# Keys of U between the steps of the expert choice, the second gathered block's stages first, and a third row buffer: one decoder layer on one core

## The chip, the core and the metric

The kernel runs on one core of one Trainium2 chip. Its time is that of one execution on the device, in microseconds (us); lower is better. The times come from repeated runs, and one further execution was recorded by the hardware profiler. The engines are named as in the profile: PE (TensorE, matmul), PEld (its weight loads), DVE (VectorE), ACT (ScalarE), POOL (GpSimd) and SP (SyncE, which here only issues transfers).

## The reference

The layer takes 512 tokens of width 2048 through three sublayers, each with a residual and a layer norm. The first mixes two sequence models (a gated linear recurrence and a forgetting attention), the second attends to a memory of 256 rows, and the third, which matters here, picks 16 of 16384 experts for each token in each of 8 heads:

```python
q = (x @ w_pq).reshape(B, S, PEER_HEADS, 2, PEER_DK // 2)
sc = jnp.einsum('bshpd,hpnd->bshpn', q, sub_keys)
top_s, top_i = lax.top_k(sc, PEER_TOPK)
...
best_s, best_pos = lax.top_k(cand_s, PEER_TOPK)
idx = jnp.take_along_axis(cand_i, best_pos, -1)
g = jax.nn.softmax(best_s, -1)
...
u = expert_u[it]
a = jnp.einsum('tkd,td->tk', u, xt)
hact = jax.nn.gelu(a, approximate=False) * gt
return jnp.einsum('tk,tkd->td', hact, expert_v[it])
```

An expert's number is made of two indices of 0 to 127: an expert is a pair of sub-keys. Each token has 128 expert rows of U and 128 of V. All data are float32.

## The kernel before, in words

**Blocks.** The 512 tokens are four blocks of 128. Block 0 goes through the whole layer's first two sublayers alone and ahead of the others; blocks 1 to 3 go through the first sublayer together. After that block 1 is taken by the object `e1` and blocks 2 and 3 by `e2` (class `Ends`: `residual`, `norm`, `attend`).

**Matrix products.** All weights come from HBM in pieces of 128 x 2048 float32, 1 MiB, loaded by `load_raw` (L150) on SP's queue into tiles named `raw`. `split_w` (L157) cuts such a piece in two halves. For each, ACT copies the half to a rounded `whi` (L147) and DVE takes the rest, `wlo` (L148); PE multiplies by both. So each half costs one copy on ACT, one split on DVE, and PE cannot start it before both.

**Two ways through the experts.** Blocks 0 and 1 are *gathered*: for each of the 128 experts of each token, POOL issues an indirect transfer of one row per token (`gather`, L981, its instruction at L983) into a `rows` tile of 128 x 2048, 1 MiB. DVE multiplies a row of U with the token and sums (L1006), or adds a row of V times its gate to the accumulator `gacc` (L1020). That makes 256 gathers per block. Tiles `rows` come from `rows_tile`, two buffers in turn. Blocks 2 and 3 are *dense*: PE multiplies all of U with the 256 tokens, one of 128 keys at a time (`stage_a`, L1249: a key is the 128 experts that share one sub-key; its result after the gelu is a tile `ga`), ACT and DVE multiply with a table of gates (`stage_h`), and PE multiplies with all of V (`stage_o`, two halves of 1024 columns for every 8 keys).

**How gathers are put in.** `add_jobs` lists the 256 jobs of a block, and `tick`, called at each split of a weight half, gives credit for a number of PE units, `set_rate` having set the jobs per unit. A job issues its gather; the gather waits for the split at which it was released (`pace`), and its use by DVE is placed `lag` splits later (`after`). Only splits release gathers: where no weights come, no gather starts.

**The stages at the end of the program**, in the order of the code: `e1.residual`, `e1.norm`, `e2.residual`, `e1.attend`, `e2.norm`, `e1.residual`, `e2.attend`, `e1.norm`, `e2.residual`; the choice of experts for block 1 (`pick1`); block 1's jobs are added with a rate of 256 in 1070 units; `e2.norm`; the choice for blocks 2 and 3 (`Choice` with `topk`, 16 pieces of weights, then sorting steps on DVE: L876 to L918); the gate table (`gbuild`, L1208 to L1240: from the chosen indices `i0T`, `i1T` DVE makes 0/1 tiles `o1` and `o0` at L1226 and L1229, ACT scales `o0` by the gate at L1232, PE multiplies them at L1233, ACT copies the product to `stage` at L1236 and stores it to HBM as `gd`); then the dense stage. In it `LOOK` = 32 keys of U run ahead of the first piece of V; after that keys and pieces of V take turns (`ahead`). Of the `ga` tiles 26 are kept; a key that runs further ahead is spilled to HBM (`gad`, 35 keys) and read back (`gb`).

**What sets the order.** The program is built with a scheduler that simulates the engines and orders each engine's instructions by it; the order of the code is only its starting point. On the chip every engine then follows its own list.

Of the kernel before, what the change touches and what calls it, by code (L numbers as in the profile page):

```python
# [21 lines left out]
P = 128  # L22
# [20 lines left out]
J = 8  # L43
GB = 8
LOOK = 32
# [4 lines left out]
def build(tc, I, out):  # L50
    nc = tc.nc
    NC_ = PKEYS
    with ExitStack() as ctx:
# [90 lines left out]
        raws = {"n": 0, "pools": [wp]}  # L144
# [5 lines left out]
        def load_raw(src, n=2048):  # L150
            raws["n"] += 1
            p = raws["pools"][raws["n"] % len(raws["pools"])]
            raw = p.tile([P, 2048], F32, tag="raw", bufs=2, name=nm("raw"))
            nc.sync.dma_start(raw[:, :n], src)
            return raw
# [709 lines left out]
        class Choice:  # L865
# [65 lines left out]
            def run(self, X2, ld):  # L931
                tp, nb = self.tp, self.nb
                for g in range(4):
# [17 lines left out]
                    for t in range(nb):  # L951
# [9 lines left out]
                        nc.scalar.copy(sc, bank)  # L961
                        self.select(t, 2 * g, sc)
# [15 lines left out]
        def rows_tile(n):  # L978
            return gat["pool"].tile([P, D], F32, tag="rows", bufs=2, name=nm(n))
# [185 lines left out]
        X1b, X1c, X2b, X2, PTb, PTc = [], [], [], [], [], []  # L1165
        drain(e1.residual(Gb, I["w_out"], True))
        e1.norm(0, X1b, pr1, False)
        drain(e2.residual(Gc, I["w_out"], True))
# [9 lines left out]
        e1.norm(1, X2b, pr1, True)  # L1178
        drain(e2.residual(PTc, Bv, False))
        with pool("pick1", side="right") as pp:  # L1180
            c = Choice(pp, pp, 1)
            drain(c.run(X2b, nc.sync))
            c.indices(1)
# [3 lines left out]
        set_rate(1070.0)  # L1187
# [4 lines left out]
        gap = ctx.enter_context(pool("gap"))  # L1192
        pre = ExitStack()
# [7 lines left out]
        def a_bank():  # L1201
            return ps.tile([P, 512], F32, tag="s2", bufs=2, name=nm("pa"))
# [8 lines left out]
        for t in range(HB):  # L1211
# [6 lines left out]
            for half in range(2):  # L1218
                stage = [gp.tile([P, 64, 64], F32, tag="stage", bufs=2, name=nm("stage")) for _ in range(2)]
                for q in range(16):  # L1220
# [10 lines left out]
                    for u in range(4):  # L1231
                        nc.scalar.activation(o0[:, u], o0[:, u], AF.Copy, scale=selT["g"][:, ta + u:ta + u + 1])  # L1232
                        nc.tensor.matmul(bank[:, u * P:(u + 1) * P], o1[:, u], o0[:, u], start=True, stop=True)  # L1233
                    bv = bank.rearrange("p (t c) -> p c t", t=4)
# [10 lines left out]
        raws["pools"].append(mn)  # L1245
        acc = [mn.tile([P, D], F32, tag=f"acc{t}", name=f"acc{t}") for t in range(HB)]
        gas, hs, gates = {}, {}, [None]

        def stage_a(c):  # L1249

            bank = a_bank()
            raw = load_raw(I["uT"][c])
            for kt in range(2):
                uh, ul = split_w(raw, kt, 2.1)
                for kk in range(8):
                    k = kt * 8 + kk
                    sl = slice(kk * P, (kk + 1) * P)
                    xh, xl = X2[k]
                    nc.tensor.matmul(bank[:, :H], uh[:, sl], xh, start=k == 0, stop=False)  # L1259
                    nc.tensor.matmul(bank[:, :H], uh[:, sl], xl, start=False, stop=False)  # L1260
                for kk in range(8):
                    k = kt * 8 + kk
                    sl = slice(kk * P, (kk + 1) * P)
                    nc.tensor.matmul(bank[:, :H], ul[:, sl], X2[k][0], start=False, stop=k == 15)  # L1264
            ga = gap.tile([P, H], F32, tag="ga", bufs=GA, name=nm("ga"))
            nc.scalar.activation(ga, bank[:, :H], AF.Gelu)
            if c in spilled:
                nc.scalar.dma_start(gad[c], ga)
            else:
                gas[c] = ga  # L1270
# [79 lines left out]
        ahead = [min(NC_, LOOK + -(-c * (NC_ - LOOK) // (NC_ - J))) for c in range(NC_)]  # L1350
        spilled = {a for c in range(NC_) for a in range(ahead[c - 1] if c else 0, ahead[c]) if a - c >= GA - 1}
# [90 lines left out]
```

## Time and profile before

| what | value |
|---|---|
| median of 3 runs | 5246.53 us (5245.74 to 5247.54) |
| the profiled execution's time | 5243.36 us |
| its span, first to last instruction | 5241.7 us |
| PE busy, share of the span | 4565.4 us, 87% |
| DVE busy | 3915.7 us, 75% |
| ACT busy | 2272.1 us, 43% |
| POOL busy | 811.7 us, 15% |
| moved by DMA | 1479.10 MB, 282 GB/s in the mean |

A busy time is read together with its place: the page's slices cut the span in 40 parts of 131 us and give the busy share in tenths. Stretches can be cut as one likes, and the waits say for whom an engine stood still. Idle time counts only on the engine that the others wait for.

### The profile page before, as it was taken

What the parts mean: (1) busy time and instruction counts of PE and PEld (TensorE: products, weight loads), DVE (VectorE), ACT (ScalarE), POOL (GpSimd) and SP (SyncE); (2) the same over time, 40 slices, a digit from 0 to 9 for tenths busy, and PEclk for the clock granted to TensorE, in tenths of its full rate; (3) what the DMA queues carried; (4) which work ended last, traced back from release to release, by engine and by line L of the source; (5) the groups of instructions that cost most, each with busy time, mean ns of one, the idle gap of its engine ahead of it and who ended that gap; (6) DMA issues with size and microseconds to landing.
All of it is one profiled execution on the core that took longest, in us unless ns stands there. A gap on an engine that the chain in (4) does not pass through costs nothing. (4 is left out here: it accounts for less than half of the span.)

```text
span 5241.7 us, 66469 instructions
## 1 busy us (share of the span) xinstructions
PE 4565.4 (87%) x25662; PEld 4021.7 (77%) x25662; DVE 3915.7 (75%) x5122; ACT 2272.1 (43%) x3129; POOL 811.7 (15%) x631
## 2 busy tenths in 40 slices
PE   7999999789999999999978887369999999999700
PEld 5888888567888998888956667359999999999600
DVE  6877777687776667776778789847787888888755
ACT  5766666543333223333334653364444444444200
POOL 0000000002222222122221001002111121212221
PEclk9999999899999999999989999689999999999955
DMA  7888888557777887776878657159998888888767
GB/s 251 307 316 316 312 314 313 207 201 267 276 272 260 309 306 283 270 276 242 312 273 338 224 209 277 49 167 341 337 337 337 338 333 336 338 332 342 272 243 253
DMA packets 265792, 1479.10 MB, mean 282 GB/s; under 512 B 26845, under 2 KB 73757, under 8 KB 97921
## 3 DMA queue, kind: packets, MB, share of 16 engines
q1 hardware_dynamic: 141696, 884.67, 45.5%
q0 software_dynamic: 81664, 561.95, 28.8%
q10 hardware_dynamic: 42112, 28.22, 1.8%
q8 instruction: 201, 3.29, 0.2%
q14 instruction: 119, 0.97, 0.0%
HBM read 1421.35 MB, written 53.39 MB: 281 GB/s over the span
## 5 line engine op out<-in xcount | busy, mean ns | idle before, releaser
L147 ACT CAST whi<-raw 128x1024 fp32r<-128x1024 f32 x1312 | 1369.4, 1051 | 1785.2 <-PE mm L179 578.4
L148 DVE TENSOR_TENSOR wlo<-raw,whi 128x1024 fp32r<-128x1024 f32 x1312 | 1590.5, 1221 | 552.4 <-ACT whi L147 423.1
L1020 DVE SCALAR_TENSOR_TENSOR gacc<-rows,dots,gacc 128x2048 f32<-128x2048 f32 x256 | 600.8, 2347 | 239.4 <-DMA rows<-in_peer_v,ei 239.0
L1006 DVE SCALAR_TENSOR_TENSOR rows<-rows,x2l 128x2048 f32<-128x2048 f32 x256 | 585.2, 2286 | 171.0 <-DMA rows<-in_peer_u,ei 170.8
L983 POOL DMA_INDIRECT rows<-in_peer_u,ei x256 | 355.3, 1388 | 1943.2 <-DVE rows L1006 755.0
L983 POOL DMA_INDIRECT rows<-in_peer_v,ei x256 | 389.8, 1523 | 1406.4 <-DVE gacc L1020 891.2
L1259 PE MATMUL pa<-Xh,whi 128*128 128x256 f32 x2048 | 503.9, 283 | 32.0 <-ACT whi L147 21.1
L1260 PE MATMUL pa<-Xl,whi 128*128 128x256 f32 x2048 | 503.2, 283 | 0.0
L179 PE MATMUL mm<-Ah,whi 128*128 128x384 f32 x1280 | 439.6, 344 | 8.2 <-DVE qk L612 3.0
L179 PE MATMUL mm<-Al,whi 128*128 128x384 f32 x1280 | 435.6, 341 | 0.0
L147 ACT CAST vh<-raw 128x1024 fp32r<-128x1024 f32 x256 | 268.1, 1052 | 353.1 <-PE mm L1311 331.0
L1259 PEld LDWEIGHTS pa<-Xh,whi 128*128 128x128 f32 x2048 | 389.9, 190 | 39.4 <-ACT whi L147 21.5
L1310 PE MATMUL mm<-vh,hph 128*128 128x512 f32 x1024 | 400.6, 392 | 0.4 <-DVE acc L1332 0.3
L1311 PE MATMUL mm<-vh,hpl 128*128 128x512 f32 x1024 | 400.6, 391 | 0.0
L1260 PEld LDWEIGHTS pa<-Xl,whi 128*128 128x128 f32 x2048 | 388.8, 190 | 6.5
L148 DVE TENSOR_TENSOR vl<-raw,vh 128x1024 fp32r<-128x1024 f32 x256 | 310.6, 1221 | 102.0 <-ACT vh L147 81.8
L223 PE MATMUL mm<-whi,Zh 128*128 128x512 f32 x832 | 333.9, 401 | 48.1 <-ACT whi L147 45.9
L224 PE MATMUL mm<-whi,Zl 128*128 128x512 f32 x832 | 331.2, 398 | 1.1 <-DVE Zl L148 1.1
L223 PE MATMUL mm<-whi,Ah 128*128 128x512 f32 x768 | 314.2, 410 | 7.5 <-ACT whi L147 7.5
L224 PE MATMUL mm<-whi,Al 128*128 128x512 f32 x768 | 311.8, 406 | 0.0
L1316 PE MATMUL mm<-vl,hph 128*128 128x512 f32 x1024 | 281.3, 392 | 9.1 <-DVE vl L148 9.1
L1264 PE MATMUL pa<-Xh,wlo 128*128 128x256 f32 x2048 | 288.7, 282 | 0.0
(399 smaller groups left out, 8360.1 us busy)
## 6 DMA issues: line engine op xcount, KB each, us to landing
raw<-in_w_in SPq DMA_DIRECT2D x256, 1024.0 KB, 5.4
raw<-in_uT SPq DMA_DIRECT2D x128, 1024.0 KB, 6.9
raw<-in_vD SPq DMA_DIRECT2D x128, 1024.0 KB, 6.7
raw<-in_w_out SPq DMA_DIRECT2D x48, 1024.0 KB, 6.2
raw<-in_peer_wq SPq DMA_DIRECT2D x48, 1024.0 KB, 4.8
raw<-in_w_xkv SPq DMA_DIRECT2D x32, 1024.0 KB, 5.6
raw<-in_w_br_ml SPq DMA_DIRECT2D x32, 1024.0 KB, 5.0
raw<-in_w_br_fx SPq DMA_DIRECT2D x32, 1024.0 KB, 4.9
```

The costliest lines, as they stand in the source:

```text
L147: nc.scalar.copy(hi, src)
L148: return nc.vector.tensor_sub(lo, src, hi.bitcast(F32))
L179: i = nc.tensor.matmul(o, w, x, start=start and s % per == 0, stop=stop and s % per == per - 1)
L223: nc.tensor.matmul(banks[t], xh[:, tt], wh[:, c], start=k == 0, stop=False)
L224: nc.tensor.matmul(banks[t], xl[:, tt], wh[:, c], start=False, stop=False)
L983: i = nc.gpsimd.indirect_dma_start(out=rows, out_offset=None, in_=I[table], in_offset=bass.IndirectOffsetOnAxis(ap=ei[t][:, k:k + 1], axis=0))
L1006: i = nc.vector.scalar_tensor_tensor(rows, rows, 1.0, tok[t]["x2l"], op0=ALU.mult, op1=ALU.mult, accum_out=d[:, k % GB:k % GB + 1])
L1020: i = nc.vector.scalar_tensor_tensor(acc, rows, d[:, GB + k % GB:GB + k % GB + 1], acc, op0=ALU.mult, op1=ALU.add)
L1259: nc.tensor.matmul(bank[:, :H], uh[:, sl], xh, start=k == 0, stop=False)
L1260: nc.tensor.matmul(bank[:, :H], uh[:, sl], xl, start=False, stop=False)
L1310: nc.tensor.matmul(banks[t][g], a[:, tt], vh[:, gs_], start=c == c0, stop=False)
L1311: nc.tensor.matmul(banks[t][g], b[:, tt], vh[:, gs_], start=False, stop=False)
```

## The change

The change has five parts.

1. The stages of block 1 come first: `e1.attend` is mixed with `e2.residual`, and `pick1` with `e2.attend`. Block 1's jobs are added ahead of the last `e2.residual`, with 1095 units in place of 1070.
2. The choice for blocks 2 and 3 stops after each of its 8 score tiles (`yield "s"`), and three keys of U (`next_a`) are put in there: 24 keys.
3. In the gate table one key is put in after every fourth of the 64 steps: 16 keys.
4. `LOOK` is 44 in place of 32, so four keys are left to run ahead after the table; 64 keys are spilled in place of 35.
5. In the dense stage every third `rows` tile comes from a third buffer in the pool `main`; in return that pool has one `raw` buffer in place of two, three in all in place of four.

```diff
-LOOK = 32
+LOOK = 44
...
-            raw = p.tile([P, 2048], F32, tag="raw", bufs=2, name=nm("raw"))
+            raw = p.tile([P, 2048], F32, tag="raw", bufs=raws["bufs"][p is not wp], name=nm("raw"))
...
                         nc.scalar.copy(sc, bank)
+                        yield "s"
                         self.select(t, 2 * g, sc)
...
         def rows_tile(n):
+            gat["n"] = gat.get("n", 0) + 1
+            if "more" in gat and gat["n"] % 3 == 0:
+                return gat["more"].tile([P, D], F32, tag="rows", bufs=1, name=nm(n))
             return gat["pool"].tile([P, D], F32, tag="rows", bufs=2, name=nm(n))
...
+        def take(g, n):
+            for _ in range(n):
+                next(g, 0)
+
         drain(e1.residual(Gb, I["w_out"], True))
         e1.norm(0, X1b, pr1, False)
-        drain(e2.residual(Gc, I["w_out"], True))
+        res = e2.residual(Gc, I["w_out"], True)
+        take(res, 4)
+        mix(e1.attend(X1b, pr1, PTb), res, 1)
+        take(res, 2)
+        drain(e1.residual(PTb, Bv, False))
+        e1.norm(1, X2b, pr1, True)
+        drain(res)
         big.close()
...
-        drain(e1.attend(X1b, pr1, PTb))
         e2.norm(0, X1c, lambda: pair(cpl, "X", 16), False)
-        drain(e1.residual(PTb, Bv, False))
-        drain(e2.attend(X1c, pr1, PTc))
+        att = e2.attend(X1c, pr1, PTc)
+        take(att, 2)
+        with pool("pick1", side="right") as pp:
+            c = Choice(pp, pp, 1)
+            mix(c.run(X2b, nc.sync), att, 4)
+            c.indices(1)
+        drain(att)
         cs.close()
...
         add_jobs(1)
-        set_rate(1070.0)
+        set_rate(1095.0)
+        drain(e2.residual(PTc, Bv, False))
         e2.norm(1, X2, lambda: pair(fpl, "X", 16), True)
...
+        def next_a():
+            stage_a(at[0])
+            at[0] += 1
...
-            drain(c.run(X2, nc.sync))
+            for w in c.run(X2, nc.sync):
+                if w == "s":
+                    for _ in range(3):
+                        next_a()
...
+                    if q % 4 == 3:
+                        next_a()
...
-        raws["pools"].append(mn)
+        gat["more"] = mn
+        raws["bufs"] = (2, 1)
+        raws["pools"] = [wp, wp, mn]
...
-        for a in range(ahead[0]):
-            stage_a(a)
+        while at[0] < ahead[0]:
+            next_a()
```

`stage_a` itself is only moved up in the code, with the tables `ahead` and `spilled`. Lines from 960 on have new numbers: L1006 and L1020 are L1010 and L1024, L1332 is L1362.

The three places below show DVE's list of instructions, before and after. DVE in the choice for blocks 2 and 3 before: only sorting steps stand there (`v`, `ix`, `rep` are the best values, their places and a copy without them; `eq` picks indices).

```order
L881 MAX_INDEX ix_25786<-v_25785,rep_25795 128x8
L879 MATCH_REPLACE rep_25801<-v_25785,sc_25783 128x128
L914 TENSOR_TENSOR eq_25769<-eq_25769,ixf_25746 128x512
L879 MATCH_REPLACE rep_25807<-v_25785,sc_25783 128x128
L880 MAX v_25785<-rep_25801 128x8
L915 TENSOR_REDUCE sel_i_4571_25073<-eq_25769 128x32
```

The same place on DVE after the change:

```order
L1010 SCALAR_TENSOR_TENSOR rows_29136,dots_29302<-rows_29136,x2l_24638 128x2048
L914 TENSOR_TENSOR eq_27911<-eq_27911,ixf_27884 128x512
L894 CAST ixf_28141<-ix_28116 128x64
L876 MAX b_28145<-cand_28143 128x8 x2
L148 TENSOR_TENSOR wlo_29395<-raw_29392,whi_29394 128x1024
L148 TENSOR_TENSOR wlo_29425<-raw_29392,whi_29424 128x1024
L915 TENSOR_REDUCE sel_i_4583_25100<-eq_27911 128x32
L1024 SCALAR_TENSOR_TENSOR gacc_24683<-rows_29272,dots_26201,gacc_24683 128x2048
```

Splits of U's keys (`wlo`) and uses of gathered rows have come between the sorting steps: from block 1's indices to the table's start DVE has 118 splits and 59 uses of rows, where it had 21 and 15.

DVE at the end of the gate table before: behind the last 0/1 tiles come the splits of U's keys, which run ahead of V.

```order
L1229 TENSOR_TENSOR o_5038_27583<-i0T,iota 128x512
L1226 TENSOR_TENSOR o_5040_27596<-i1T,iota 128x512
L1229 TENSOR_TENSOR o_5041_27598<-i0T,iota 128x512
L148 TENSOR_TENSOR wlo_27687<-raw_27684,whi_27686 128x1024
L148 TENSOR_TENSOR wlo_27715<-raw_27684,whi_27714 128x1024
L1283 TENSOR_TENSOR ga_27681<-ga_27681,G_29690 128x256
```

The same place on DVE after the change:

```order
L1278 TENSOR_TENSOR o_5359_30120<-i0T,iota 128x512
L1275 TENSOR_TENSOR o_5361_30133<-i1T,iota 128x512
L1278 TENSOR_TENSOR o_5362_30135<-i0T,iota 128x512
L1313 TENSOR_TENSOR ga_25427<-ga_25427,G_30493 128x256
L1313 TENSOR_TENSOR ga_25491<-ga_25491,G_30493 128x256
L148 TENSOR_TENSOR wlo_30290<-raw_30287,whi_30289 128x1024
```

The keys that ran ahead here are gone from this place: 77 more splits of keys stand ahead of the table's first rows and three within its first part; between the last of these and its end there is neither a split nor a gathered row, as before.

DVE around the last pieces of V before (`vl` is the split of V; `acc` the dense blocks' sum):

```order
L1006 SCALAR_TENSOR_TENSOR rows_37753,dots_37192<-rows_37753,x2l_25146 128x2048
L148 TENSOR_TENSOR vl_41672<-raw_41669,vh_41671 128x1024
L148 TENSOR_TENSOR vl_41688<-raw_41669,vh_41687 128x1024
L1020 SCALAR_TENSOR_TENSOR gacc_25209<-rows_37808,dots_36312,gacc_25209 128x2048
L1332 TENSOR_TENSOR acc_27617<-acc_27617,mm_41563 128x512
L1006 SCALAR_TENSOR_TENSOR rows_37866,dots_37192<-rows_37866,x2l_25146 128x2048
```

The same place on DVE after the change:

```order
L148 TENSOR_TENSOR vl_41759<-raw_41756,vh_41758 128x1024
L148 TENSOR_TENSOR vl_41775<-raw_41756,vh_41774 128x1024
L1362 TENSOR_TENSOR acc_30219<-acc_30219,mm_41650 128x512
L1362 TENSOR_TENSOR acc_30219<-acc_30219,mm_41651 128x512
L1362 TENSOR_TENSOR acc_30220<-acc_30220,mm_41652 128x512
L1362 TENSOR_TENSOR acc_30220<-acc_30220,mm_41653 128x512
```

Before, 63 uses of gathered rows stood behind the last split of V. Now none does: all 512 stand ahead of it, 195 of them behind the gate table (241 before).

More of the change, by code (lines that the diff above doesn't have):

```diff
@@ L143, in build @@
         ticks = []
-        raws = {"n": 0, "pools": [wp]}
+        raws = {"n": 0, "pools": [wp], "bufs": (2, 2)}
         def split(hi, lo, src):
@@ L1171, in build @@
         cpl = cs.enter_context(pool("x1c", side="right"))
-        drain(e1.attend(X1b, pr1, PTb))
         e2.norm(0, X1c, lambda: pair(cpl, "X", 16), False)
-        drain(e1.residual(PTb, Bv, False))
-        drain(e2.attend(X1c, pr1, PTc))
+        att = e2.attend(X1c, pr1, PTc)
[5 more added lines that the diff above has]
+        drain(att)
         cs.close()
         fpl = ctx.enter_context(pool("x2c", side="right"))
[L1178 to L1183, printed above, removed]
         while state["done"] < len(jobs):
@@ L1192, in build, with a_bank, stage_a @@
         gap = ctx.enter_context(pool("gap"))
+        gas, at = {}, [0]
+        def a_bank():
+            return ps.tile([P, 512], F32, tag="s2", bufs=2, name=nm("pa"))
+        ahead = [min(NC_, LOOK + -(-c * (NC_ - LOOK) // (NC_ - J))) for c in range(NC_)]
+        spilled = {a for c in range(NC_) for a in range(ahead[c - 1] if c else 0, ahead[c]) if a - c >= GA - 1}
+        def stage_a(c):
+            bank = a_bank()
+            raw = load_raw(I["uT"][c])
+            for kt in range(2):
+                uh, ul = split_w(raw, kt, 2.1)
+                for kk in range(8):
+                    k = kt * 8 + kk
+                    sl = slice(kk * P, (kk + 1) * P)
+                    xh, xl = X2[k]
+                    nc.tensor.matmul(bank[:, :H], uh[:, sl], xh, start=k == 0, stop=False)
+                    nc.tensor.matmul(bank[:, :H], uh[:, sl], xl, start=False, stop=False)
+                for kk in range(8):
+                    k = kt * 8 + kk
+                    sl = slice(kk * P, (kk + 1) * P)
+                    nc.tensor.matmul(bank[:, :H], ul[:, sl], X2[k][0], start=False, stop=k == 15)
+            ga = gap.tile([P, H], F32, tag="ga", bufs=GA, name=nm("ga"))
+            nc.scalar.activation(ga, bank[:, :H], AF.Gelu)
+            if c in spilled:
+                nc.scalar.dma_start(gad[c], ga)
+            else:
+                gas[c] = ga
+        def next_a():
+            stage_a(at[0])
+            at[0] += 1
         pre = ExitStack()
@@ L1196, in build @@
             c = Choice(pp, tp, 2)
-            drain(c.run(X2, nc.sync))
+            for w in c.run(X2, nc.sync):
+                if w == "s":
+                    for _ in range(3):
+                        next_a()
         sel = c.sel
         state["lag"] = 3
-        def a_bank():
-            return ps.tile([P, 512], F32, tag="s2", bufs=2, name=nm("pa"))
         def o_bank():
@@ L1244, in build @@
         mn = ctx.enter_context(pool("main"))
-        raws["pools"].append(mn)
+        gat["more"] = mn
+        raws["bufs"] = (2, 1)
+        raws["pools"] = [wp, wp, mn]
         acc = [mn.tile([P, D], F32, tag=f"acc{t}", name=f"acc{t}") for t in range(HB)]
[L1247 to L1270, printed above, removed]
+        hs, gates = {}, [None]
         def stage_h(c):
@@ L1347, in fin @@
                 nc.sync.dma_start(out[(HB + t) * P:(HB + t + 1) * P, sl], acc[t][:, sl])
-        ahead = [min(NC_, LOOK + -(-c * (NC_ - LOOK) // (NC_ - J))) for c in range(NC_)]
-        spilled = {a for c in range(NC_) for a in range(ahead[c - 1] if c else 0, ahead[c]) if a - c >= GA - 1}
-        for a in range(ahead[0]):
-            stage_a(a)
+        while at[0] < ahead[0]:
+            next_a()
         for c0 in range(0, NC_, J):
```

## The prediction

> **What bounds the kernel now.** I read the page's slices first, then busy time in stretches that I cut at the landmarks of the code, then the waits and the DMA queues in the longest stretch. The slices (131 us each) show two holes:
>
> ```profile
> PE   7999999789999999999978887369999999999700
> DVE  6877777687776667776778789847787888888755
> DMA  7888888557777887776878657159998888888767
> ```
>
> TensorE is full nearly everywhere except in slices 24 to 26 and in the last three; DVE is full in the first hole and half idle in the second. These rows cut the second half of the program; the columns are the stretch, its length, then PE, weight loads, DVE, ACT and POOL busy (x instructions), granted clock, DMA share and GB/s:
>
> ```profile
> 2771.00:3177.00 406.00, 357.46 (x1671) 278.98 (x1670) 338.94 (x594) 220.11 (x290) 24.30 (x17) 0.95 0.69 250
> 3177.00:3345.00 168.00, 81.11 (x607) 78.44 (x605) 162.83 (x536) 33.99 (x42) 18.10 (x16) 0.74 0.48 178
> 3345.00:3505.00 160.00, 98.21 (x549) 90.21 (x550) 85.03 (x137) 115.39 (x386) 0.94 (x1) 0.82 0.40 114
> 3550.00:4900.00 1350.00, 1349.89 (x8712) 1231.46 (x8711) 1093.57 (x1105) 575.72 (x737) 258.68 (x166) 1.00 0.89 336
> 4942.00:5242.00 300.00, 8.15 (x28) 6.30 (x28) 178.91 (x143) 6.30 (x11) 66.67 (x63) 0.52 0.70 246
> ```
>
> The first holds the mixed stages of projection, norms and memory attention. The second is the choice of experts for the last two blocks: DVE 162.83 of 168 us, so DVE sets it. The third is the gate table, where no engine is full: it is a chain of DVE, ACT and PE. The fourth is the dense stage over U and V: PE 1349.89 of 1350 us. In the last PE is done and only gathers run: POOL's instructions there are the gathers, 63, and 166 in the dense stage, that is 1350 / 166 = 8.13 us per gather. What sets that pace is in the waits of the dense stage (total us, times, longest):
>
> ```profile
> POOL rows L983 <- DVE gacc L1020: 537.8, 83, 12.8
> POOL rows L983 <- DVE rows L1006: 524.0, 77, 14.1
> ```
>
> POOL waits for DVE to give a row buffer back; with two buffers and the use standing some splits later in DVE's queue, gathers fall behind, and 63 are left when TensorE stops. The last matmul, and the uses of rows in the 290 us from there to the end:
>
> ```profile
> L1316 PE MATMUL mm<-vl,hph x1024: 387/389/796, 3694.6 to 4952.3; 128*128 128x512 f32 x171
> L1020 DVE SCALAR_TENSOR_TENSOR gacc<-rows,dots,gacc 128x2048 f32<-128x2048 f32 x38 | 89.3, 2350 | 94.5 <-DMA rows<-in_peer_v,ei 94.5
> L1006 DVE SCALAR_TENSOR_TENSOR rows<-rows,x2l 128x2048 f32<-128x2048 f32 x25 | 57.3, 2291 | 18.4 <-DMA rows<-in_peer_u,ei 18.2
> ```
>
> The kernel is thus bound by TensorE up to 4952 us and by leftover gathers for 290 us.
>
> **The change, part by part.** *The tail goes.* In the changed order no gather's use stands behind the last split of V (63 did). Up to 290 us are at stake; what remains after the last matmul is the end of the two dense blocks: accumulation, statistics and four passes per block, of which these are the long ones,
>
> ```profile
> 5227.14 4.87 DVE L1032 SCALAR_TENSOR_TENSOR acc<-acc,fst,lw 128x1024 f32<-128x1024 f32 x4 [1.44 <-DMA lw<-in_ln_w]
> 5233.11 4.87 DVE L1033 SCALAR_TENSOR_TENSOR acc<-acc,fst,lw 128x1024 f32<-128x1024 f32 x4 [1.09 <-DMA lw<-in_ln_b]
> ```
>
> with the stores about 25 us. But those uses now stand ahead of splits that TensorE needs, so late gathers stop TensorE.
>
> *The choice grows.* Landmarks: block one's indices are ready, the gate table begins, the main stream of keys begins:
>
> ```profile
> L969 DVE CAST ei<-ef x1: 226/226/226, 3177.2 to 3177.2; 128x128 int32<-128x128 f32 x1
> L1217 DVE COPY i0T<-mm x2: 279/286/293, 3345.5 to 3415.5; 128x128 f32<-128x128 f32 x2
> 3498.44 0.58 PE L1259 MATMUL pa<-Xh,whi 128*128 128x256 f32 x1 [7.39 <-ACT whi L147]
> ```
>
> By the order 20 splits of weights stand behind the cast of the indices that stood ahead of it, and the second norm of the last two blocks too (8 of the 16 passes in the third row, as many of about 0.5 us, and its small ones: 16 us, an estimate). Uses and splits cost this in the choice,
>
> ```profile
> L1006 DVE SCALAR_TENSOR_TENSOR rows<-rows,x2l 128x2048 f32<-128x2048 f32 x14 | 31.9, 2279 | 2.2 <-DMA rows<-in_peer_u,ei 2.2
> L148 DVE TENSOR_TENSOR wlo<-raw,whi 128x1024 fp32r<-128x1024 f32 x21 | 25.3, 1214 | 2.8 <-ACT whi L147 2.8
> L148 DVE TENSOR_TENSOR Xl<-f,Xh 128x512 fp32r<-128x512 f32 x16 | 10.6, 684 | 0.7 <-ACT Xh L147 0.7
> ```
>
> So the indices come 20 x 1.2 + 16 = 40 us earlier, at 3137. From there to the gate table DVE now has 118 splits (39 keys of U are among them, where one was) and 59 gather uses in place of 21 and 15. Before: 162.8 busy = 31.9 + 25.3 + 105.6 for the rest. After: 59 x 2.35 + 118 x 1.214 + 105.6 + 16 = 139 + 143 + 122 = 404 us. The 39 keys are 39 x 5.65 = 220 us of PE (below) beside it, and hide. DVE was 97% busy in the old choice; with splits that wait for ACT and gathers I take 96%: 404 / 0.96 = 421, so the gate table begins at 3558, 213 us later than now. The stages ahead of the choice are only interleaved anew, block one's attention with block two's products: the same work, with 49 us in which PE idles now (406 - 357.46) to win or as much to lose; I take none.
>
> *The gate table stays as it is.* The code puts 16 keys between its quarters, but the order moves all but three halves of them ahead of it: it stands alone again, with no gather. It takes 3498.4 - 3345.5 = 153 us. Its chain,
>
> ```profile
> DVE o L1226 <- PE mm L1233: 59.5, 42, 7.2
> PE mm L1233 <- ACT o L1232: 42.6, 29, 6.6
> ```
>
> is untouched, and the two gathers and three splits at its start (8 us) fit DVE's 75 idle us. The last store and load of the table then meet 2.8 keys of ready matmuls; I add 3 us. The dense stage begins at 3558 + 153 + 3 = 3714.
>
> *The dense stage shrinks for PE.* Prices come from a stretch with keys alone, and the counts in the long stretch:
>
> ```profile
> 3550.00:3600.00 50.00, 50.00 (x425) 50.00 (x424) 39.75 (x40) 23.19 (x31) 10.41 (x6) 1.00 0.93 357
> L1259 PE MATMUL pa<-Xh,whi 128*128 128x256 f32 x1936 | 471.8, 281 | 0.0
> L1310 PE MATMUL mm<-vh,hph 128*128 128x512 f32 x967 | 377.8, 391 | 0.1
> ```
>
> A key is 48 matmuls at 50 / 425 = 0.118, so 5.65 us; the 1936 / 16 = 121 keys take 684 of the 1350, the 967 / 8 = 121 pieces of V the other 666, 5.51 each. By the order 41 keys are done before; 87 x 5.65 + 128 x 5.51 = 1197 us.
>
> *But DMA does not shrink with it.* Of the 256 gathers 195 remain (the order has 61 before), 63 of them no longer in the tail. The queues of the dense stage (packets, MB, share of 16 engines):
>
> ```profile
> q1 hardware_dynamic: 48485, 273.74, 53.3%
> q0 software_dynamic: 23904, 174.07, 34.1%
> q10 hardware_dynamic: 5040, 4.59, 1.0%
> ```
>
> Per MB: 0.533 x 1350 / 273.74 = 2.63 us on q1, 2.645 on q0, 2.94 on q10. After: 212 weight loads of 1.049 MB, 64 pieces of the table, 64 spilled keys read back (35 before) and constants are 254 MB, 668 us; 195 gathers 204.5 MB, 541 us; 48 spills 6.3 MB, 19 us; about 1230 us of full engines against 1197 of PE. Full they never are. The best stretches:
>
> ```profile
> 3900.00:3950.00 50.00, 50.00 (x312) 45.10 (x311) 41.62 (x43) 22.84 (x30) 9.66 (x6) 1.00 0.95 350
> 2820.00:2840.00 20.00, 18.18 (x78) 14.01 (x77) 16.77 (x12) 6.76 (x7) 4.75 (x4) 1.00 0.98 390
> ```
>
> I take the 50 us one, 0.95. The last nine pieces of V have no gather beside them (50 us at PE's pace, 25 us of DMA), so the stage takes (1230 - 25) / 0.95 + 50 = 1318 us; at the 0.89 of now 1404, at 0.98 1280. The Trainium skill ("DMA: Bandwidth & Descriptors", Where 436 GB/s comes from) says that HBM's 358 GB/s per core binds such loads; by it 465 MB would take 1299 us. The 390 GB/s above is over that figure, if for 20 us only.
>
> *Third row buffer, one weight buffer less.* By the order five to six splits of PE's pace (2.8 us each, 14 to 17 us) lie between the split that releases a gather and its use, against this from issue to landing:
>
> ```profile
> DMA to landing us min/median/max: 5.4/8.5/11.8
> rows<-in_peer_u,ei POOLq DMA_INDIRECT x83, 8.4
> raw<-in_vD SPq DMA_DIRECT2D x124, 1024.0 KB, 6.8
> gad<-ga ACTq DMA_DIRECT2D x35, 128.0 KB, 5.2
> ```
>
> That is covered. Three buffers for the weights instead of four: 3 x 5.6 = 16.8 us per turn, of which landing is 6.8 and the two splits about 5; covered by 5 us, and gone when landing doubles. The 29 more spills are issued on ACT's queue, and each holds the one free key buffer for 5.2 us, under a key's 5.65 on PE. On SP's queue the table's loads stand behind 41 keys' loads and ahead of V's, where they wait for the table's last store as they do now. I charge nothing beyond the DMA term.
>
> **Sum.** 3714 + 1318 + 25 = 5057 us of span, against 5241.7. The profiled execution took 1.7 us more than its span and the median of the runs lies 3.2 us above it: **5062 us**, 184 us or 3.5% faster. Runs of this kernel differ by 2 us; I call 0.2% (10 us) the least that can be told.
>
> **The rivals.** *DMA does not bind.* If the engines run all through as in the 390 GB/s stretch, TensorE sets the dense stage: 3714 + 1197 + 25 + 5 = 4941 us. For it: the 0.98 was seen. Against: it asks for 465 / 1197 = 388 GB/s for 1.2 ms, where 357 is the best 50 us of the dense stage quoted. The Trainium skill (same page, Measured) has 425 GB/s for one core with its neighbour idle, which would give this case; no row here comes near it.
>
> *The choice becomes a queue of waiting gathers.* There the order leaves only three splits, 3 x 421 / 118 = 10.7 us, between release and use, and a landing of 8.4 with 1.1 on POOL fills 9.5:
>
> ```profile
> L983 POOL DMA_INDIRECT rows<-in_peer_u,ei x14 | 16.0, 1144 | 347.2 <-DVE ei L969 290.1 <-DVE rows L1006 18.1 <-DVE v L880 9.5
> ```
>
> If landing goes to the 11.8 of the row above, each of 59 uses waits 2.2 us and DVE, TensorE's source of splits, with it: +130 us, 5192. At the 338.94 / 406 = 83% that DVE reaches where the stages are mixed it is 404 / 0.83 = 487, +66 us, 5128.
>
> *Gathers keep their pace, and the kernel gets slower.* If 8.13 us per gather is what the loaded DMA queues give and not the buffers, the uses ahead of V's splits now hold TensorE: 195 x 8.13 = 1585, and 3714 + 1585 + 50 + 25 + 5 = 5379. It decides from the point where the dense stage fills all time up to now's end: 5241.7 - 25 - 3714 - 50 = 1453, 7.45 us per gather. For it: DMA was 89% busy already. Against: 63 gathers alone took 290 us, 4.6 each with two buffers, and DVE waited 1.7 us in all for landings in the dense stage:
>
> ```profile
> DVE rows L1006 <- DMA rows<-in_peer_u,ei: 1.7, 3, 1.3
> ```
>
> **How the numbers follow.** Forecast (dense stage bound by DMA between 0.98 and 0.89, 5020 to 5145, choice within 20 us): 0.62. DMA does not bind: 0.12. The choice waits, 5145 to 5235: 0.19. Slower: 0.05, and 0.02 for no change, a tail won and given back. The range reaches to the first rival's time and to the waiting choice's: 4940 to 5190. Faster 0.93, same 0.02, slower 0.05.
>
> **What would show it.** Right: no stretch at the end with DVE at half and PE at zero; 40 keys of U before the gate table; the table's 153 us at about 3560 with PE half idle and no gather; a dense stage with PE at 90% and DMA at 0.93 or more. A gate table that begins after 3620 shows the choice too cheap in my sum; PE at 99% in the dense stage shows the first rival; DVE waiting for landings by hundreds of us, with DMA below 0.89, the last. The forecast is wrong if the dense stage takes under 1230 or over 1410 us.

## The result and the profile after

The changed kernel takes 5028.3 us (median of 4 runs, 5018.7 to 5033.7) against 5247.0 of the kernel before beside it (4 runs, 5245.7 to 5258.6): ratio 0.9576, 95% interval 0.9557 to 0.9596, so 4.2% or 219 us faster. The forecast was 5062 us. The profiled execution took 5018.7 us with a span of 5017.0.

The slices of the page (125 us each) against the three shown of before:

```profile
PE   7999999889999999999997888888769999999998
DVE  6877777678877666677676879899658888889887
DMA  6888888656777788777687865788669999999996
```

The zeros of TensorE at the end are gone, and the DMA engines stand at 9 in slices 30 to 38 (counted from 0, as in the prediction). The hole that is left in TensorE's row, slices 28 and 29, is the gate table. The landmarks, with the same meaning as before: block one's indices, the start of the gate table, its last matmul, the first and the last matmul of V.

```profile
L970 DVE CAST ei<-ef x2: 219/223/227, 1192.8 to 3116.2; 128x128 int32<-128x128 f32 x2
L1266 DVE COPY i0T<-mm x2: 281/286/291, 3551.6 to 3626.2; 128x128 f32<-128x128 f32 x2
L1282 PE MATMUL mm<-o,o x512: 270/341/583, 3556.6 to 3702.4; 128*128 128x128 f32 x171
L1340 PE MATMUL mm<-vh,hph x1024: 386/389/506, 3744.7 to 4996.3; 128*128 128x512 f32 x171
L1346 PE MATMUL mm<-vl,hph x1024: 387/389/505, 3747.4 to 4997.4; 128*128 128x512 f32 x171
```

Cut at these landmarks (length, then PE, weight loads, DVE, ACT and POOL busy, granted clock, DMA share, GB/s):

```profile
3116.00:3552.00 436.00, 378.54 (x2876) 361.35 (x2875) 393.36 (x744) 166.50 (x211) 80.05 (x61) 0.95 0.80 298
3552.00:3705.00 153.00, 100.26 (x603) 91.44 (x602) 89.86 (x139) 115.33 (x388) 6.00 (x2) 0.88 0.41 124
3705.00:3745.00 40.00, 22.35 (x138) 21.90 (x139) 18.90 (x26) 11.27 (x18) 5.99 (x4) 0.74 0.93 320
3745.00:4945.00 1200.00, 1148.14 (x6880) 1007.97 (x6879) 1060.45 (x1062) 473.42 (x622) 299.87 (x191) 1.00 0.96 373
4945.00:5001.00 56.00, 51.85 (x235) 42.13 (x233) 38.02 (x48) 21.61 (x22) 0.00 (x0) 0.99 0.46 170
```

In the dense stage POOL issues 191 gathers in 1200 us, 6.3 us each (8.13 before), the DMA engines are busy 0.96 of the time at 373 GB/s (0.89 and 336), and TensorE, which had no idle time there, now has 52 us of it. What the gathers wait for has changed too (total us, times, longest; dense stage of after):

```profile
POOL rows L987 <- DVE vl L148: 316.8, 73, 10.9
POOL rows L987 <- DVE wlo L148: 263.7, 54, 9.5
POOL rows L987 <- DVE gacc L1024: 143.7, 29, 10.4
POOL rows L987 <- DVE rows L1010: 134.3, 29, 8.5
```

The first two rows are the splits that release a gather by plan, 580 us; the last two are a row buffer that is not yet given back, 278 us, where those two rows held 1062 before. So it is mostly the plan that now sets the gathers' pace, and no longer the buffers.

### The profile page after: what moved, and what is told of

It reads as the page before. It is cut to its first block, busy times and chain, and to the rows that moved or that the text cites. A ratio compares the mean times of both kernels' runs of the same rounds, so it can differ in the third digit from the quotient of the medians.

```text
span 5017.0 us, 66345 instructions
## 1 busy us (share of the span) xinstructions
PE 4599.9 (92%) x25662; PEld 4024.0 (80%) x25662; DVE 3908.1 (78%) x5122; ACT 2257.2 (45%) x3125; POOL 824.2 (16%) x631
## 5 line engine op out<-in xcount | busy, mean ns | idle before, releaser
L1010 DVE SCALAR_TENSOR_TENSOR rows<-rows,x2l 128x2048 f32<-128x2048 f32 x256 | 585.2, 2286 | 164.5 <-DMA rows<-in_peer_u,ei 164.2
L1024 DVE SCALAR_TENSOR_TENSOR gacc<-rows,dots,gacc 128x2048 f32<-128x2048 f32 x256 | 600.5, 2346 | 137.7 <-DMA rows<-in_peer_v,ei 137.5
L987 POOL DMA_INDIRECT rows<-in_peer_u,ei x256 | 388.4, 1517 | 1800.1 <-DVE wlo L148 800.9
L987 POOL DMA_INDIRECT rows<-in_peer_v,ei x256 | 369.2, 1442 | 1250.6 <-DVE wlo L148 666.9
L1229 PEld LDWEIGHTS pa<-Xh,wlo 128*128 128x128 f32 x2048 | 262.9, 191 | 47.0 <-DVE wlo L148 46.5
```

The costliest lines, as they stand in the source:

```text
L987: i = nc.gpsimd.indirect_dma_start(out=rows, out_offset=None, in_=I[table], in_offset=bass.IndirectOffsetOnAxis(ap=ei[t][:, k:k + 1], axis=0))
L1010: i = nc.vector.scalar_tensor_tensor(rows, rows, 1.0, tok[t]["x2l"], op0=ALU.mult, op1=ALU.mult, accum_out=d[:, k % GB:k % GB + 1])
L1024: i = nc.vector.scalar_tensor_tensor(acc, rows, d[:, GB + k % GB:GB + k % GB + 1], acc, op0=ALU.mult, op1=ALU.add)
```

## The experiments

Theory A, the forecast's: leftover gathers held the end; with them inside the program the dense stage is held by the DMA engines at about full use; work that is moved ahead lengthens the choice by what it holds of VectorE, and the gate table stays. Theory B takes the gain from keys of U moved into the holes, a relief for TensorE. Each run below stands beside runs of the kernel before on the same chip.

**1. One part at a time.** Four kernels, run together. The changed kernel with the row buffers and weight buffers as they were:

```diff
 def rows_tile(n):
-    gat["n"] = gat.get("n", 0) + 1
-    if "more" in gat and gat["n"] % 3 == 0:
-        return gat["more"].tile([P, D], F32, tag="rows", bufs=1, name=nm(n))
...
-gat["more"] = mn
-raws["bufs"] = (2, 1)
-raws["pools"] = [wp, wp, mn]
+raws["pools"].append(mn)
```

> The changed kernel with its third row buffer taken out again (two buffers for gathered rows, four for weights); the block-one-first order and the keys between the steps stay. Theory A (the kernel was held by gathers that fall behind, and the row buffer is what lets them keep up; keys ahead only move work from the dense stage into the choice): by its order 54 uses of rows stand behind the last split of V, so the dense stage ends by TensorE at about 3710 + 1205 = 4915 and 54 x 4.6 us of gathers follow: about 5200 us, nearly all of the gain gone. Theory B (the gain comes from filling TensorE's holes in the choice and the gate table with keys): about 5060 us, most of the gain kept.

The kernel before with the new order of the stages alone (part 1 of the change):

```diff
+res = e2.residual(Gc, I["w_out"], True)
+take(res, 4)
+mix(e1.attend(X1b, pr1, PTb), res, 1)
...
+    mix(c.run(X2b, nc.sync), att, 4)
...
-set_rate(1070.0)
+set_rate(1095.0)
```

> The kernel before with the new order of block one's stages alone (no keys in the choice or the table, LOOK 32, two row buffers). Theory A: gathers start some 60 us earlier, 56 uses stand behind the last split in place of 63, about 5230 us. Theory B: no hole is filled, about 5240 us. A third view, that the earlier start of block one's gathers is the gain: 60 to 100 us, 5150 to 5190 us.

The kernel before with the keys between the steps alone (parts 2 to 4):

```diff
-LOOK = 32
+LOOK = 44
...
+    for w in c.run(X2, nc.sync):
+        if w == "s":
+            for _ in range(3):
+                next_a()
...
+                    if q % 4 == 3:
+                        next_a()
```

> The kernel before with the keys between the steps alone (LOOK 44, 24 keys in the choice, 16 in the table; old order of the stages, two row buffers). Theory A: the choice grows by about 200 us of DVE work, the dense stage shrinks by as much on TensorE, 60 uses stand behind the last split: about 5215 us. Theory B: 100 to 150 us faster, 5100 to 5150 us.

The kernel before with the third row buffer and one weight buffer less alone (part 5, the reverse of the first diff):

> The kernel before with the third row buffer alone (one weight buffer less; no keys, old order of the stages). By its order no use stands behind the last split. Theory A: the dense stage starts at 3505 as before and is bound by the transfers: 292 MB of loads at 2.59 us, 253 MB of gathers at 2.53 and 13 us of spills are 1408 us of full DMA engines, at 0.96 some 1485 us; about 5015 to 5040 us, the whole gain of the change. Theory B: gathers catch up, but TensorE's holes stay: 5120 to 5180 us.

A fifth, run later, splits part 5 again: three weight buffers in place of four, and still two row buffers.

```diff
-gat["more"] = mn
 raws["bufs"] = (2, 1)
 raws["pools"] = [wp, wp, mn]
```

> The kernel before with three weight buffers in place of four and still two row buffers: the other half of the exchange that the run with three row buffers alone made. Theory A (the third row buffer is the gain, the weight buffer given up costs nothing): within 10 us of the kernel before. Rival B (fewer weight loads in flight leave the gathers a larger share of the DMA engines, which is where a part of the gain comes from): 20 to 100 us faster. Third view (TensorE waits for weights): 10 to 50 us slower.

Measured (each ratio is against the kernel before that ran beside it, 5247.0 to 5251.7 us; the right column counts, in DVE's list of instructions, the uses of gathered rows behind the last split of V):

| kernel | us | ratio, 95% interval | uses behind |
|---|---|---|---|
| before | 5247.0 | 1 | 63 |
| all parts but 5 | 5183.9 | 0.9874 (0.9843 to 0.9904) | 54 |
| part 1 alone | 5233.6 | 0.9974 (0.9959 to 0.9989) | 56 |
| parts 2 to 4 alone | 5187.7 | 0.9889 (0.9857 to 0.9922) | 60 |
| part 5 alone | 5042.8 | 0.9600 (0.9566 to 0.9633) | 0 |
| one weight buffer less alone | 5202.6 | 0.9906 (0.9891 to 0.9921) | 53 |
| all parts | 5028.3 | 0.9576 (0.9557 to 0.9596) | 0 |

Part 5 alone brings 4.0 of the 4.2%; the ratio of all parts to part 5 alone, 0.9576 / 0.9600, cannot be told from one. Theory B expected 5120 to 5180 us of part 5 alone and falls; A's range there, 5015 to 5040, is missed by 3 us. A's other figures (5200, 5230 and 5215 us for the rows above it) are off by 4 to 27 us, the most for the keys alone, which gain 1.1% where it gave them 0.6. The third view of part 1, that the earlier start of the gathers is the gain (5150 to 5190 us), falls too. The dense stage of part 5 alone, cut as the row of before:

```profile
3550.00:4900.00 1350.00, 1292.62 (x8237) 1162.11 (x8237) 1183.97 (x1151) 534.07 (x703) 364.11 (x224) 1.00 0.96 370
```

It has 224 gathers where before has 166, the DMA share 0.96 of the changed kernel, and TensorE has 57 us of idle time. With all parts but 5 the same stage, cut behind the table there, keeps the picture of before:

```profile
3750.00:4900.00 1150.00, 1150.00 (x6988) 1030.78 (x6987) 938.34 (x988) 487.90 (x631) 205.38 (x134) 1.00 0.89 336
4942.00:5180.00 238.00, 0.00 (x0) 0.00 (x0) 143.33 (x116) 3.76 (x8) 46.82 (x50) 0.50 0.74 255
```

134 gathers in 1150 us are 8.58 us each, and 50 are issued in the tail of 238 us.

Theory A expected the weight buffer given up to cost nothing, within 10 us; it gains 49 us, which lies in the range of rival B. In size it answers to the order: 10 uses fewer stand behind the last split (53 for 63), at the 4.6 us of a tail gather 46 us. Two row buffers and three weight buffers still give 7.7 us per gather in the dense stage (175 in 1350 us):

```profile
3550.00:4900.00 1350.00, 1344.43 (x8709) 1226.24 (x8709) 1111.96 (x1115) 568.21 (x738) 273.11 (x175) 1.00 0.90 343
```

Taken in this order, about 0.9 of part 5's 4.0% lies in the weight buffer, and 1 - 0.9600 / 0.9906 = 3.1% in the row buffer; a third row buffer beside four weight buffers wasn't run. Why the planner sets those ten uses earlier when a weight buffer is missing wasn't tried. Rival B's reason, that the loads crowd the gathers less, isn't excluded: a DMA share of 0.90 for 0.89 speaks neither way.

**2. What holds the dense stage.** Two kernels take load off one side each. The first halves the gathers of V for the second block:

```diff
+short = t == 1 and table == "peer_v"
-out=rows, out_offset=None, in_=I[table],
+out=rows[:, :1024] if short else rows, out_offset=None,
+in_=I[table].rearrange("r (a c) -> (r a) c", a=2) if short else I[table],
```

> The changed kernel, in which the 64 gathers of V's rows for the second gathered block fetch half a row (512 KB in place of 1,024 KB) and VectorE reads the half twice, so that its work keeps its size; that block's result is of the wrong rows. It takes some 32 MB off the transfers, nearly all of it behind 3,745 us. Theory A (the dense stage is held by the DMA engines, 0.96 of their time used): at 2.5 to 2.6 us a MB the stage loses up to 80 us, of which TensorE (busy 1,148 of 1,200 us there) lets 40 to 60 go: 4,968 to 4,990 us. Rival B (the stage is held by TensorE's or VectorE's work, the transfers only fill what is left): within 10 us of the changed kernel, 5,018 to 5,038 us.

The expectation miscounts: the second block gathers 128 rows tiles of V, not 64, and 103 of them lie in this kernel's stretch from 3745 to 4900, so 54 MB are taken off there, not 32. The second takes work off TensorE:

```diff
-for kk in range(8):
+for kk in range(8 if c < 41 else 0):
     ...
     nc.tensor.matmul(bank[:, :H], ul[:, sl], X2[k][0], ...)
```

> The changed kernel without the third product (the low part of the weights times the high part of X, 16 matmuls of 128 columns a key) in the 87 keys of U from number 41 on, so that the result is less exact; all transfers, splits and VectorE's work stay. TensorE loses 87 x 16 = 1,392 matmuls, by the page's 118 ns some 160 us, nearly all of it behind 3,745 us. Theory A (the dense stage is held by the DMA engines): the stage stays, 0 to 40 us shorter: 4,988 to 5,028 us. Rival B (held by TensorE): 110 to 160 us shorter: 4,870 to 4,920 us.

Halved rows: 4983.1 us, ratio 0.9497 (0.9483 to 0.9512), in the range of A. One product less: 5000.2 us, 0.9523 (0.9507 to 0.9538), in the range of A and 80 us above B's. The changed kernel, run beside them: 5030.5 us, 0.9594 (0.9579 to 0.9609), as expected of it:

> The changed kernel once more, to stand beside the other runs of this call on the same chip: 5,018 to 5,038 us by every theory.

The dense stage of the changed kernel in that run, of halved rows, and of one product less:

```profile
3745.00:4900.00 1155.00, 1106.07 (x6646) 972.07 (x6646) 1019.37 (x1027) 456.82 (x602) 325.66 (x187) 1.00 0.96 372
```

```profile
3745.00:4900.00 1155.00, 1137.14 (x6910) 1014.05 (x6910) 1055.80 (x1065) 484.98 (x631) 433.90 (x193) 1.00 0.90 342
```

```profile
3745.00:4900.00 1155.00, 1010.33 (x5435) 858.54 (x5434) 1036.40 (x1042) 466.97 (x611) 363.57 (x190) 0.97 0.96 379
```

Less to transfer: the DMA share falls to 0.90, TensorE goes from 49 us of idle time to 18, and the time falls by 47 us. Less to multiply: the DMA share stays at 0.96, TensorE's idle time triples to 145 us, and of about 160 us of matmuls taken away the time shows 30. From the first matmul of V to the last the three take 1252, 1198 and 1231 us. So TensorE's work is not what holds the stage, and transfers taken away shorten it until TensorE, with 18 us of idle time, is nearly full: TensorE is the next bound, some 50 us behind.

Two things stay open. TensorE's busy time in the whole kernel falls by 125 us and not by 160 (4608.8 to 4483.6), since its granted clock in the stage is 0.97 for 1.00. And the waits don't name the transfers (total us, times, longest, in the same stretch; the first two rows are the changed kernel's, the last two those of one product less):

```profile
PE mm L1340 <- ACT vh L147: 11.7, 13, 1.4
ACT vh L147 <- DMA raw<-in_vD: 51.6, 26, 4.8
```

```profile
PE mm L1340 <- ACT vh L147: 125.4, 76, 2.2
ACT vh L147 <- DMA raw<-in_vD: 14.3, 6, 3.9
```

With TensorE relieved it waits more for ACT's copies of V, but ACT waits less for V's pieces to land, and VectorE waits for landings 3 to 5 us in both. VectorE is busy 0.90 of the stretch there (1036 of 1155 us), the share that it has in the choice, where it sets the time. So in this kernel the order of ACT's and VectorE's work may hold the stage as much as the transfers do; no run takes work off those two. That the transfers hold the stage rests on the halved rows alone, whose order differs a little as well (two uses and three splits more in the choice).

**3. Is there room in the gate table?** The table shows VectorE busy 90 of 153 us and the DMA engines 0.41. Four kernels put work into it. The first holds the splits of the table's 16 keys behind the first step of their quarter; in the changed kernel they run ahead of the table:

```diff
-def split_w(raw, i, cost):
+def split_w(raw, i, cost, dep=None):
     s = split(hi, lo, raw[:, i * 1024:(i + 1) * 1024])
+    if dep is not None:
+        after(s, dep)
...
-                        next_a()
+                        next_a(od)
```

> The changed kernel with the splits of the 16 keys of the gate table held behind the first step of their quarter on VectorE, so that they no longer run before the table. Theory A (the work that is moved ahead of the table lengthens the choice by what it holds of VectorE, and the table has room): 16 keys of some 2.4 us on VectorE leave the choice, 35 to 42 us; the table, in which VectorE was busy 90 of 153 us, grows by 0 to 20 us: 15 to 40 us faster than the changed kernel, 4,988 to 5,013 us. Rival B (the gate table's chain of steps waits for VectorE, so each key's splits lengthen it by as much as the choice gets shorter): within 8 us of the changed kernel.

The next two let 16 gathers more go inside the table, with their uses. The order then sets 10 and 5 splits of keys more into it as well, with their casts and matmuls:

```diff
-nc.vector.tensor_tensor(o0, selT["i0"][:, ta:ta + 4] ...
+od = nc.vector.tensor_tensor(o0, selT["i0"][:, ta:ta + 4] ...
+if q % 4 == 1:
+    tick(od, 1.0 / state["rate"])
...
+left = len(jobs) - state["done"]
+state["rate"] *= left / (left + 16)
```

> The changed kernel with 16 gathers more let go inside the gate table, one behind the first step of every fourth quarter, and the pace behind the table lowered so that the rest spreads as before. By the order 29 uses of rows now stand inside the table (2 before), 302 ahead of it (315) and 14 fewer behind it; 13 splits stand inside (3). Theory A (the choice is held by VectorE, the dense stage by the DMA engines, which idle in the table): the choice loses 13 x 2.35 + 10 x 1.2 = 43 us of VectorE, 46 us at its pace; the table's VectorE work goes from 90 to 166 us, so the table to some 170 to 185 us, 20 to 35 longer; the dense stage loses 14.7 MB, 37 us: 30 to 65 us faster than the changed kernel, 4,965 to 5,000 us. Rival B (as in the run with the keys in the table, the table grows by as much as the choice gets shorter, and the dense stage gives nothing): 5,020 to 5,045 us.

In the second of them the condition is `if t == 1 and q % 2 == 1:`.

> The same, with the 16 gathers let go in the second half of the gate table alone. By the order 15 uses stand inside the table, 308 ahead of it and 6 fewer behind it; 8 splits stand inside. Theory A: the choice loses 7 x 2.35 + 5 x 1.2 = 22 us of VectorE, 24 at its pace; the table gains 37 us of VectorE's work in 60 idle, 0 to 20 us longer; the dense stage loses 6.3 MB, 16 us: 20 to 40 us faster than the changed kernel, 4,988 to 5,010 us. Rival B: within 10 us of the changed kernel, 5,018 to 5,040 us.

The last is the first of these two with `bufs=4` in place of `bufs=2` for the 0/1 tiles `o1` and `o0`.

> The kernel with 16 gathers more let go all through the gate table, with four buffers for each of the two one-hot tiles of its steps in place of two. By the order 19 uses and some 16 splits stand inside the table, 321 uses up to its end (331 with two buffers, 317 in the changed kernel), so VectorE has 90 + 17 x 2.35 + 13 x 1.2 = 146 us of work there. Theory A (with two buffers the table is a ring of VectorE, ScalarE, TensorE in which every us added on VectorE lengthens it; more buffers let VectorE run ahead and use its idle time): the table takes 155 to 170 us where it took 225: 4,985 to 5,010 us. Rival B (added work counts in full however many buffers there are): the table takes some 205 us: 5,030 to 5,045 us.

Measured: keys in the table 5052.2 us, ratio 0.9634 (0.9621 to 0.9648), slower than the changed kernel; gathers all through 5042.5, 0.9597 (0.9583 to 0.9611); late gathers 5035.9, 0.9585 (0.9572 to 0.9598), neither to be told from it; gathers with four tiles 5016.1, 0.9544 (0.9528 to 0.9561). The choice and the table of the changed kernel that ran beside the keys, cut at its own landmarks:

```profile
3127.80:3563.70 435.90, 376.72 (x2859) 359.11 (x2858) 392.60 (x742) 166.34 (x210) 86.21 (x60) 0.95 0.80 297
3563.70:3714.60 150.90, 101.68 (x617) 92.83 (x615) 90.40 (x141) 116.28 (x388) 2.08 (x2) 0.88 0.41 126
```

With the keys in the table:

```profile
3131.30:3487.30 356.00, 290.30 (x2160) 274.94 (x2158) 325.74 (x690) 129.24 (x164) 65.67 (x46) 0.91 0.74 275
3487.30:3715.10 227.80, 171.37 (x1254) 165.30 (x1254) 149.78 (x190) 150.49 (x430) 32.98 (x15) 0.87 0.58 198
```

With gathers all through it, with late gathers, and with gathers and four tiles:

```profile
3136.60:3524.80 388.20, 342.22 (x2627) 326.96 (x2626) 352.08 (x711) 154.26 (x194) 59.64 (x46) 0.96 0.76 281
3524.80:3749.90 225.10, 144.49 (x851) 136.07 (x851) 162.03 (x195) 131.77 (x405) 52.08 (x32) 0.71 0.72 243
```

```profile
3123.70:3537.20 413.50, 361.19 (x2745) 344.96 (x2744) 371.03 (x726) 160.11 (x203) 70.96 (x53) 0.94 0.78 289
3537.20:3721.90 184.70, 122.45 (x728) 114.34 (x726) 126.84 (x168) 124.64 (x396) 18.73 (x16) 0.74 0.61 194
```

```profile
3146.70:3533.80 387.10, 341.05 (x2623) 327.14 (x2623) 352.12 (x711) 153.94 (x194) 61.49 (x46) 0.95 0.76 281
3533.80:3712.70 178.90, 122.18 (x853) 118.77 (x851) 139.78 (x180) 126.17 (x404) 36.89 (x22) 0.82 0.73 246
```

Each choice and table against the changed kernel's 435.9 and 150.9 us:

| kernel | choice | table | VectorE's work in the table | ACT's | splits of keys and uses of rows in it (3 and 2 in the changed kernel) |
|---|---|---|---|---|---|
| keys in the table | -79.9 | +76.9 | +59.4 | +34.2 | 30 and 14 |
| gathers all through | -47.7 | +74.2 | +71.6 | +15.5 | 13 and 29 |
| late gathers | -22.4 | +33.8 | +36.4 | +8.4 | 8 and 15 |
| gathers, four tiles | -48.8 | +28.0 | +49.4 | +9.9 | 13 and 19 |

The choice does what theory A says: it gives back what VectorE is relieved of, 48 and 22 us in the two kernels with gathers where 46 and 24 were expected. The table does not. With two tiles it grows by 1.04 us (gathers all through) and 0.93 us (late ones) for each us that is put on VectorE, though VectorE idles 60 of 151 us there, and both kernels end in the range of rival B. The keys put the most work on ACT, and the table grows by more than VectorE's part. Rival B's mechanism held there, but not its 8 us: V's first matmul comes 54 us behind the table's last (42 in the changed kernel), and the time is 22 us longer. The waits in the changed kernel's table point to the reason (DVE, PE and ACT in turn):

```profile
DVE o L1275 <- PE mm L1282: 56.8, 44, 7.3
PE mm L1282 <- ACT o L1281: 35.9, 36, 6.6
ACT o L1281 <- DVE o L1278: 10.2, 11, 1.5
```

VectorE waits for a tile that TensorE gives back, TensorE for ACT's scaling, ACT for VectorE: a ring with two places. By this reading what stands between two steps on VectorE delays the ring, and the idle time is waiting inside it. Four places take the price down to 28.0 / 49.4 = 0.57 us per us, which fits. That is nearer to theory A, which had 155 to 170 us for the table, than to rival B with 205; its 179 us lie outside both, and so does its time of 5016 us (4985 to 5010 and 5030 to 5045). Four places leave less in the table as well (19 uses for 29), so only the price per us compares, and that not fully: the lengths of the table's matmuls differ between these kernels too (last section).

This last kernel has the lowest ratio of all that compute the whole layer, 0.9544 against 0.9594 and 0.9576 for the changed kernel, each beside other runs of the kernel before; its interval stands clear of that of the first and touches that of the second. From block one's indices to the end its profiled run takes 5028.3 - 3146.7 = 1881.6 us, those of the changed kernel 5028.8 - 3127.8 = 1901.0 and 5017.0 - 3116.2 = 1900.8: 19 us less. The stages ahead, which are the same code, gave indices at 3116 to 3147 us in these runs, a spread larger than the gain.

## Why the forecast held, step by step

It was right in sign and size, 34 us too high. The steps are off by 3 to 26 us with errors of both signs, so a part of the closeness is luck:

| step | forecast us | measured us |
|---|---|---|
| block one's indices at | 3137 | 3116 |
| choice | 421 | 435 |
| gate table and lead to 3705 | 156 | 153 |
| dense stage from there to the last matmul | 1318 | 1292 |
| end | 25 | 20 |
| span | 5057 | 5017 |

- **The tail goes.** Right; of 290 us behind the last matmul 20 are left. But the forecast took this from the order of the whole change and never said which part empties it. It is the row buffer with the weight buffer given up: without part 5, 54 uses stay behind. The sentence that nothing is charged for the third buffer "beyond the DMA term" priced its cost and passed over its gain, 3.1 of the 4.2%.
- **The indices.** The forecast counted 40 us of work moved behind them and nothing for idle time. The kernel with part 1 alone has them at 3134.9, as counted; 3116 is the early end of the 3116 to 3147 us at which they come in the profiled runs of the changed kernel and of its variants, all of which have the same code ahead of them. Why they vary wasn't tried.
- **The choice.** VectorE's work was 393.4 us where 404 were counted, at 0.90 of the time where 0.96 was taken: 435 for 421. The waits that the second rival named are in it, in small:

```profile
L1010 DVE SCALAR_TENSOR_TENSOR rows<-rows,x2l 128x2048 f32<-128x2048 f32 x36 | 82.2, 2283 | 22.1 <-DMA rows<-in_peer_u,ei 22.0
L1024 DVE SCALAR_TENSOR_TENSOR gacc<-rows,dots,gacc 128x2048 f32<-128x2048 f32 x23 | 53.8, 2340 | 6.7 <-DMA rows<-in_peer_v,ei 6.6
L148 DVE TENSOR_TENSOR wlo<-raw,whi 128x1024 fp32r<-128x1024 f32 x118 | 142.1, 1213 | 10.1 <-ACT whi L147 8.2 <-ACT f L774 1.8
```

  22.0 + 6.6 for landings and 10.1 for splits are 39 of the 42 us in which VectorE idles; the rival's price was 2.2 us per use, measured are 28.6 / 59 = 0.5.
- **The gate table.** Its length was right, but the reason that two uses and three splits "fit DVE's 75 idle us" was not: from the table's start to its last matmul it takes 150.8 us where before it took 145.3, which is most of those 8 us, and in section 3 work put on VectorE there lengthened the table by about its own size.
- **The lead.** 3 us were added for it. From the last matmul of the table to the first of V 42 us pass, and TensorE is busy 22 of the 40 in the row above. In that time ACT waits 18.3 us for the table's last store (`gd<-stage`) and VectorE 18.0 for its load (`G<-gd`), with too few keys' splits ready for TensorE. It may cost less than it looks, since the DMA engines are 0.93 busy in it and load for the stage behind it; that wasn't tried.
- **The dense stage.** Too dear by 2%. The DMA share is 0.96 where 0.95 was taken, and the halved rows speak for the cause; but TensorE is busy 0.96 of the stage where the forecast's sign was 0.90, so it is nearer to being the bound than the forecast had it. The price of a MB was the mis-sized term:

```profile
q1 hardware_dynamic: 47039, 239.49, 51.7%
q0 software_dynamic: 27572, 200.72, 42.3%
```

  0.517 x 1200 / 239.49 = 2.59 us on q1 and 2.53 on q0, against 2.63 and 2.645 taken from before: on 254 and 204.5 MB 10 and 24 us. A price that was read at a share of 0.89 overstated that at 0.96. With these prices the sum gives (1196 - 25) / 0.96 + 50 = 1270 us, 22 below the measured 1292: other terms were too small, such as the bytes (470 MB by the three rows above from 3705 on, 465 counted) and the end (56 us for 50).
- **The rivals.** *DMA does not bind* needed TensorE to set the stage; a product less on TensorE gave 30 of 160 us, so its work alone doesn't. *Gathers keep their pace* is refuted by 6.3 us per gather. The Trainium skill ("DMA: Bandwidth & Descriptors", Where 436 GB/s comes from) puts loads from HBM at 358 GB/s per core; 373 over 1200 us are above it, and the measured figure decides.

What the keys between the steps are worth is hidden in the forecast's sum. Part 5 alone has its indices at 3175.5 us, the table at 3347.5 and ends at 5043.0; all parts have 3116.2, 3551.6 and 5017.0. So parts 1 to 4 bring the indices 59 us earlier, lengthen the choice by 263 and shorten what follows by 230. Work goes from the dense stage into the choice, which VectorE holds, at about the same price: by the order the run with the keys in the table has 31 splits and 14 uses fewer in the choice, 31 x 1.21 + 14 x 2.32 = 70 us of VectorE, 78 at its 0.90, and the choice is 80 us shorter; the 29.5 transfers that go with them (half of 31, and 14), of 1.049 MB each, would take 82 us of the dense stage at 2.55 us per MB and a share of 0.96, an estimate.

## What to carry to other kernels

Count what waits behind the last work of the bound engine, and ask what sets its pace: here two buffers did, a third in exchange for a weight buffer brought nearly all of the gain, and the other four parts, 40 keys moved into holes among them, brought next to nothing beside it. Idle time of an engine in a chain isn't room by itself: with two tiles between the engines it was none here, with four about half. Before you put work there, compare its idle time with its waits for the other members of the ring. Where two bounds lie close together, here 50 us of 1250, taking load off one of them gains only the distance to the other, so weigh each move by the engine that sets the stage it leaves and the one that sets the stage it enters.

## What the runs showed that was not expected

- The DMA engines moved 373 GB/s for 1200 us on one core, at a share of 0.96, and a MB got cheaper as the share rose (2.645 us at 0.89, 2.53 at 0.96 on the gathers' queue), while the landing of a gather rose from a median of 8.5 to 9.5 us:

```profile
DMA to landing us min/median/max: 5.4/9.5/13.9
```

- One weight buffer less made a kernel 49 us faster; in its order ten uses of rows stand earlier, which at the price of a gather in the tail is 46 us.
- The granted clock in the gate table fell to 0.71 and 0.74 with gathers in it, where the changed kernel had 0.88, the keys 0.87 and the gathers with four tiles 0.82. The table's matmuls then took a median of 421 and 377 ns in place of 342, but 275 with four tiles, so the mean clock alone doesn't set their length. Whether TensorE's waits lower the clock or a lower clock draws out the ring, and how much of the longer table is due to it, stays open.
- The three runs of before that were shown with its profile differ by 2 us; 13 others, run together, went from 5234.5 to 5260.1 us. So 0.2% is too fine for single runs, and 5016.1 against 5030.5 us, which didn't run together, is a hint.
